# Output projection of a hybrid decoder layer as seven products of halves (Strassen's scheme), with the memory branch in front of it in an order by keys

## Chip, core and metric

The kernel runs on one core of one Trainium2 chip. The metric is the device time of one execution in microseconds (us), lower is better. The engines are TensorE (PE: matmuls; PEld: its weight loads), VectorE (DVE), ScalarE (ACT), GpSimd (POOL) and SyncE (SP), each with a queue of its own that runs in order. SP issues nearly all DMAs.

## What is computed

One decoder layer for 512 tokens and 1024 channels: three branches (SSD, RG-LRU, memory cross-attention) are projected, gated and added; the sum goes through the output projection, the residual is added, and a last RMSNorm is taken. The part that the change touches:

```python
merged = (gates[:, :, 0] * (y_ssd @ w_br_ssd[l])
          + gates[:, :, 1] * (y_lru @ w_br_lru[l])
          + gates[:, :, 2] * (y_mem @ w_br_mem[l]))
x = x + merged @ w_out[l]            # (512, 1024) @ (1024, 1024)
...
return rms_norm(x, final_g)
```

## The kernel before

All matrix products are made in three passes: each operand is split into a high part of type fp32r and the rest (`hi`, a cast on ACT; `lo`, a subtraction `src - hi` on POOL or DVE), and TensorE adds up hi x hi, hi x lo and lo x hi (`mm3`, L279 to L281; `rows_proj`, L300 to L302). One matmul has 128 contracted channels, 128 stationary and 512 moving columns.

Weights come through `WeightStream`: a list of pieces of 128x1024 elements, each loaded by a DMA on SP into one of four `raw` tiles (L83), cast on ACT into `whi` (L100) and subtracted into `wlo` on POOL, POOL, DVE in turn (L102). There are three buffers for `whi` and `wlo`; taking piece i (`ws.next()`) writes out the split of piece i+2 ahead of the matmuls of piece i.

The stage that is changed is the last one. Everything in front of it (SSD, RG-LRU, attention, the sigmoid gates) is the same instruction stream on every engine in both kernels.

- **Memory branch** (L1093 to L1105): for each of eight tiles `ct` of 128 channels TensorE makes 24 matmuls into one PSUM bank (`pj`, four of them). DVE multiplies the result by its gate (L1098, one operand in PSUM, one in SBUF) and adds it to `merged` (L1099, both in SBUF). ACT casts `merged` to its high part (L199), DVE subtracts the low part (L200, both operands in SBUF). The weights are eight pieces of `w_br_mem`.
- **Output projection** (L1128 to L1146): `merged` holds channels on partitions and 512 tokens along the row, so it is the stationary side, four chunks of 128 tokens. The left half of the 1024 output columns is made by `rows_proj` from four pieces of `w_out` (96 matmuls); the right half chunk by chunk, 24 matmuls each, from `woh` and `wol`, which lie in the buffers of the normed input (`hTh`, `hTl`), free by then. That is 8 x 24 = 192 matmuls.
- **End** (`half_done`, L1114): per chunk and half DVE adds the residual (L1117), ACT squares and sums (L1119), DVE multiplies by the gain (L1125); after the right half POOL takes the power -0.5 (L1124), DVE and ACT scale one half each (L1143, L1145), and SP sends both out (L1144, L1146).

The order here is the scheduler's. The RG-LRU stage ahead of it has its order by hand: steps are put into an `Order` list with a key (a time planned by the author) and written out sorted by key, between `tc.manual_schedule()`; the planned lengths in it are keys and hold nothing back.

Of the kernel before, what the change touches and what calls it, by code (L numbers as in the profile page):

```python
# [38 lines left out]
class WeightStream:  # L39
# [50 lines left out]
    def advance(self, upto):  # L90
        while self.n_sub <= min(upto, len(self.subs) - 1):
# [4 lines left out]
            src = self.raw_tiles.pop(i)  # L96
# [52 lines left out]
def kernel(  # L149
# [850 lines left out]
    with tc.tile_pool(name="att", bufs=1, reuse_waits="tile") as ap, ExitStack() as ctx2:  # L1000
# [42 lines left out]
        with tc.tile_pool(name="att2", bufs=1, reuse_waits="tile") as bp:  # L1043
# [48 lines left out]
            mhl = []  # L1092
            for ct in range(KD):  # L1093
                hi, lo = ws.next()
                pt = ps("pj", 4)
# [12 lines left out]
        xr = ap.tile([P, NCH, D], F32, tag="tbx", name="xr")  # L1108
        nc.sync.dma_start(xr, x2.rearrange("(c p) d -> p c d", p=P))
        gb = op.tile([P, D], F32, name="fgb")  # L1110
        nc.sync.dma_start(gb, final_g.partition_broadcast(P))
        stats = [op.tile([P, 4], F32, name=f"ost{c}") for c in range(NCH)]

        def half_done(c, i, pt):  # L1114

            xc, st = xr[:, c, i * 512:(i + 1) * 512], stats[c]
            V.scalar_tensor_tensor(xc, pt, 0.5, xc, op0=ALU.mult, op1=ALU.add)  # L1117
            junk = op.tile([P, 512], BF16, tag="junk", name=f"oj{c}_{i}")
            A.activation(junk, xc, AF.Square, accum_out=st[:, 0:1])  # L1119
            if i == 0:  # L1120
                V.tensor_scalar(st[:, 1:2], st[:, 0:1], 1.0 / D, EPS, op0=ALU.mult, op1=ALU.add)
            else:
                V.scalar_tensor_tensor(st[:, 2:3], st[:, 0:1], 1.0 / D, st[:, 1:2], op0=ALU.mult, op1=ALU.add)
                G.tensor_tensor(st[:, 3:4], st[:, 2:3], mhalf, op=ALU.pow)  # L1124
            V.tensor_mul(xc, xc, gb[:, i * 512:(i + 1) * 512])  # L1125

        pts = rows_proj(lambda k: tuple(m[:, k % 4, :] for m in mhl[k // 4]), NCH, KD)
        woh = hp.tile([P, KD, 512], F32R, tag="hTh", name="woh")  # L1128
        wol = hp.tile([P, KD, 512], F32R, tag="hTl", name="wol")
        for r in range(4):  # L1130
            wr = rawp.tile([P, 1024], F32, tag="raw", name=f"rawo{r}").rearrange("p (k c) -> p k c", k=2)
# [44 lines left out]
```

## Time and profile before

| | |
|---|---|
| median of 3 runs | 969.37 us (967.92 to 970.47) |
| the profiled execution | 968.6 us, of which 966.6 us are its span |
| TensorE busy in the span | 98% |
| the changed stage | 872.5 to 966.6 us of the span: 94.1 us |
| of it memory branch | 872.5 to 916.1 |
| of it output projection | 916.1 to 959.7 |
| of it after the last matmul | 959.7 to 966.6 |

A row of a timeline gives start and length of one instruction (or of some alike, xN) in us, its engine, line, operation, out<-in and shape, and in brackets how long the engine had been idle and what ended that. The start is when the instruction is at the head of its queue with its semaphores there; if it then has to wait for something else, its length grows. Matmuls overlap: a length of 0.39 with starts 0.227 apart.

### The profile page before, as it was taken

To read this page: it belongs to the slowest core of one execution; us is meant where nothing else is said; L and a number is where in the kernel's file an instruction comes from. 1 tells how busy PE (TensorE), PEld (TensorE's weight loads), DVE (VectorE), ACT (ScalarE), POOL (GpSimd) and SP (SyncE) were. 2 spreads that over 40 slices of the span, in tenths; PEclk is the share of its full clock that TensorE was granted. 3 is DMA by queue.
4 is the path that set the end of the run, shared out by engine and by line. 5 is a ranking of instruction groups with operands and counts; after the bars stand their busy time and mean duration, and the time that the engine had idled before them with its cause. 6 is when DMAs were issued, how large, how long until landed. Compare 5 with 4: busy or idle time off the path is not lost.

```text
span 966.6 us, 11884 instructions
## 1 busy us (share of the span) xinstructions
PE 946.8 (98%) x4504; PEld 783.0 (81%) x4504; DVE 611.6 (63%) x932; ACT 446.0 (46%) x673; POOL 281.5 (29%) x156
## 2 busy tenths in 40 slices
PE   8998999999999999999999999999999999999997
PEld 5787778888888888888888887888888988888885
DVE  4398999868688867555648486867465254314643
ACT  5234435544443433331594967768324354332322
POOL 4333315233323323222002011120383442123321
PEclk9999999999999999999999999999999999999999
DMA  7324324333333333324553837464353454233332
GB/s 250 99 68 132 110 66 141 89 110 108 99 103 112 113 94 113 88 69 108 140 155 87 216 112 189 123 169 134 96 165 98 141 159 110 57 99 90 119 119 87
DMA packets 138141, 114.49 MB, mean 118 GB/s; under 512 B 8741, under 2 KB 121701, under 8 KB 138086
## 3 DMA queue, kind: packets, MB, share of 16 engines
q1 hardware_dynamic: 138084, 113.75, 40.6%
q8 instruction: 35, 0.57, 0.2%
q14 instruction: 20, 0.16, 0.1%
q10 hardware_dynamic: 2, 0.00, 0.0%
HBM read 98.99 MB, written 2.16 MB: 105 GB/s over the span
## 4 chain that ended last, share of the span: by engine, by line
PE 84%; DVE 10%; DMA 2%; ACT 1%; issue 1%; POOL 0%; POOLq 0%; SPq 0%; ACTq 0%; DVEq 0%
PE pj L280 21%; PE pj L279 21%; PE pj L281 21%; PE pj L302 2%; PE pj L300 2%; PE pj L301 2%; PE yd L652 2%; DMA m<-acs_d 2%; DVE m L606 2%; DVE cv_xs L310 1%; PE pj L418 1%; PE st L279 1%; PE pj L420 1%; PE pj L419 1%; DVE wlo L102 1%
## 5 line engine op out<-in xcount | busy, mean ns | idle before, releaser
L102 POOL TENSOR_TENSOR wlo<-raw,whi 128x1024 fp32r<-128x1024 f32 (+1 forms) x88 | 211.0, 2399 | 429.3 <-ACT whi L100 419.9
L100 ACT CAST whi<-raw 128x1024 fp32r<-128x1024 f32 (+1 forms) x152 | 155.5, 1025 | 201.9 <-PE pj L280 99.2
L279 PE MATMUL pj<-hTh,whi 128*128 128x512 f32 x624 | 244.6, 392 | 0.2 <-DVE z L317 0.2
L281 PE MATMUL pj<-hTh,wlo 128*128 128x512 f32 x624 | 244.1, 391 | 0.0
L280 PE MATMUL pj<-hTl,whi 128*128 128x512 f32 x624 | 243.8, 391 | 0.0
L279 PEld LDWEIGHTS pj<-hTh,whi 128*128 128x128 f32 x624 | 117.3, 188 | 24.5 <-DVE z L317 0.4
L281 PEld LDWEIGHTS pj<-hTh,wlo 128*128 128x128 f32 x624 | 117.2, 188 | 24.4
L280 PEld LDWEIGHTS pj<-hTl,whi 128*128 128x128 f32 x624 | 117.2, 188 | 24.2
L102 DVE TENSOR_TENSOR wlo<-raw,whi 128x1024 fp32r<-128x1024 f32 x64 | 84.6, 1322 | 55.3 <-ACT whi L100 55.3
L281 PE MATMUL pj<-yTh,wlo 128*128 128x512 f32 x128 | 51.0, 398 | 0.0
L280 PE MATMUL pj<-yTl,whi 128*128 128x512 f32 x128 | 50.5, 394 | 0.0
L279 PE MATMUL pj<-yTh,whi 128*128 128x512 f32 x128 | 50.5, 398 | 0.0
L606 DVE TENSOR_SCALAR m<-m,acs 128x128 f32<-128x128 f32 x128 | 37.7, 362 | 7.5 <-DMA m<-acs_d 7.5
L310 DVE SCALAR_TENSOR_TENSOR cv_xs<-pj,par,cv_xs 128x511 f32<-128x511 f32 (+2 forms) x48 | 35.6, 741 | 9.0 <-ACT cv_xs L307 8.8
L301 PE MATMUL pj<-wlo,hTh 128*128 128x512 f32 x96 | 37.7, 392 | 0.0
L300 PE MATMUL pj<-whi,hTh 128*128 128x512 f32 x96 | 37.5, 398 | 0.0
L302 PE MATMUL pj<-whi,hTl 128*128 128x512 f32 x96 | 37.5, 393 | 0.0
L281 PE MATMUL pj<-lyh,wlo 128*128 128x512 f32 x96 | 37.4, 390 | 0.0
L280 PE MATMUL pj<-lyl,whi 128*128 128x512 f32 x96 | 37.4, 390 | 0.0
L279 PE MATMUL pj<-lyh,whi 128*128 128x512 f32 x96 | 37.4, 390 | 0.0
L652 PEld LDWEIGHTS yd<-xdt,m 128*128 128x128 f32 x256 | 34.5, 191 | 2.4
L652 PE MATMUL yd<-xdt,m 128*128 128x64 f32 x256 | 33.1, 266 | 0.0
(373 smaller groups left out, 1787.1 us busy)
## 6 DMA issues: line engine op xcount, KB each, us to landing
raw<-in_w_in_dram SPq DMA_DIRECT2D x92, 512.0 KB, 3.9
m<-acs_d SPq DMA_DIRECT2D x16, 512.0 KB, 3.7
raw<-in_w_br_ssd_dram SPq DMA_DIRECT2D x16, 512.0 KB, 3.3
raw<-in_w_kv_dram SPq DMA_DIRECT2D x16, 512.0 KB, 3.8
raw<-in_w_br_lru_dram SPq DMA_DIRECT2D x16, 384.0 KB, 3.6
raw<-in_w_br_mem_dram SPq DMA_DIRECT2D x8, 512.0 KB, 3.8
b<-lx SPq DMA_DIRECT2D x8, 384.0 KB, 4.6
ri<-g SPq DMA_DIRECT2D x8, 384.0 KB, 3.7
```

The lines of the kernel that those rows point to most:

```text
L100: self.nc.scalar.copy(hi, src)
L102: lo_engine.tensor_sub(lo, src, hi)
L279: T.matmul(dst, lhsT=lh, rhs=rh, start=(i == 0), stop=False)
L280: T.matmul(dst, lhsT=lh, rhs=rl, start=False, stop=False)
L281: T.matmul(dst, lhsT=ll, rhs=rh, start=False, stop=(i == n - 1))
L300: T.matmul(pts[c], lhsT=lh[:, sl], rhs=hi[:, k2, :], start=first, stop=False)
L301: T.matmul(pts[c], lhsT=lh[:, sl], rhs=lo[:, k2, :], start=False, stop=False)
L302: T.matmul(pts[c], lhsT=ll[:, sl], rhs=hi[:, k2, :], start=False, stop=last)
L310: V.scalar_tensor_tensor(acc[:, k:S], pt[:, 0:S - k], wcol(t), acc[:, k:S], op0=ALU.mult, op1=ALU.add)
L418: T.matmul(zps[c], lhsT=hTh[:, k, sl], rhs=zh[:, k2, :], start=(k == 0), stop=False)
L606: V.tensor_scalar(m[:, h, :], m[:, h, :], acs[:, r0 + h:r0 + h + 1], 0.0, op0=ALU.subtract, op1=ALU.min)
L652: T.matmul(pd[:, h * 64:(h + 1) * 64], lhsT=e["m%d" % c][:, h, :], rhs=e["xdt%d" % c][:, h * 64:(h + 1) * 64], start=True, stop=True)
```

## The change

The 512x1024 matrix `merged` and the 1024x1024 matrix `w_out` are cut into halves both ways: A11, A12 (first 256 tokens), A21, A22 (last 256), B11 to B22. In place of eight products of blocks there are seven, with sums of blocks as operands (Winograd's form): S1 = A21+A22, S2 = S1-A11, S3 = A11-A21, S4 = A12-S2; T1 = B12-B11, T2 = B22-T1, T3 = B22-B12, T4 = T2-B21. The products, in their order: A11 B11, S3 T3, S1 T1, A12 B21, S2 T2, S4 B22, A22 T4. Each is two banks of 128 tokens by 512 columns, made in two parts of 12 matmuls: 7 x 24 = 168 matmuls. The results are added into the residual `xr` quarter by quarter, some by way of a tile `u`.

- `w_out` is no longer streamed: four DMAs of 1 MB bring it as fp32 into the buffers of `hTl` and `hTh` (`wcol`), T1 to T4 are made there in place or in `t3`, and the fourteen half operands run through the weight stream as pieces without a load (`add_kept`): `whi` on ACT, `wlo` on POOL for the first half and on DVE for the second.
- `half_split` follows each memory tile on DVE and ACT: for tiles 0 to 3 the split of A11's part and S3 with its split, for tiles 4 to 7 S1, S2, S4 and three splits. The tiles come in the order 0, 4, 1, 5, 2, 6, 3, 7.
- The whole stage is put into an `Order` list by keys and written out in `manual_schedule`.
- The last scaling is cut at column 640 (DVE) and the rest (ACT), and ACT issues the DMA of its part itself.

The core of the diff:

```diff
+    def add_kept(self, make, k, w, lo_engine):
+        self.lo_of[len(self.subs)] = lo_engine
+        self.subs.append((make, k, w))
...
-            src = self.raw_tiles.pop(i)
+            src = self.subs[i][0]() if callable(self.subs[i][0]) else self.raw_tiles.pop(i)
...
+    for i, ct in enumerate(ct_order):
+        ws.lo_now = (V, G)[i % 2]
+        ws.add_cols(w_mem2, ct * P, 1)
...
+    for i, name in enumerate(("b11", "t3", "t1", "b21", "t2", "b22", "t4")):
+        for r in range(2):
+            ws.add_kept(lambda name=name, r=r: wo[name](r), 2, 512, (G, V)[r])
...
+        def wo_load(l, j):
+            if j == 1:
+                wcol.append(hp.tile([P, KD, 512], F32, tag=("hTl", "hTh")[l], name=f"wcol{l}"))
+            nc.sync.dma_start(wcol[1 - l][:, 4 * j:4 * j + 4, :],
+                              w_out2[j * 512:(j + 1) * 512, l * 512:(l + 1) * 512].rearrange("(k p) c -> p k c", p=P))
...
+        def sum_t3(r):
+            G.tensor_sub(t3[:, 2 * r:2 * r + 2, :], b(1, 1, r), b(0, 1, r))
+        def sum_t1(r):
+            G.tensor_sub(b(0, 1, r), b(0, 1, r), b(0, 0, r))
+        def make_t2(r):
+            V.tensor_sub(b(0, 0, r), b(1, 1, r), b(0, 1, r))
+            return b(0, 0, r)
+        def make_t4(r):
+            (G, V)[r].tensor_sub(b(1, 0, r), b(0, 0, r), b(1, 0, r))
+            return b(1, 0, r)
...
+        def half_split(ct):
+            m = merged[:, ct, :]
+            t0, t1 = m[:, 0:HALF_T], m[:, HALF_T:S]
+            if ct < 4:
+                split(a11[:, 0, ct, :], a11[:, 1, ct, :], t0, V)
+                d = op.tile([P, HALF_T], F32, tag="sd", name=f"sd{ct}")
+                V.tensor_sub(d, t0, t1)
+                split(s3[:, 0, ct, :], s3[:, 1, ct, :], d, V)
+                return
+            j = ct - 4
+            d = op.tile([P, 2, HALF_T], F32, tag="ss", name=f"ss{ct}")
+            V.tensor_add(d[:, 0, :], merged[:, j, HALF_T:S], t1)
+            V.tensor_sub(d[:, 1, :], d[:, 0, :], merged[:, j, 0:HALF_T])
+            split(s12h[:, j], s12l[:, j], d, V)
+            d4 = op.tile([P, HALF_T], F32, tag="sd", name=f"sd{ct}")
+            V.tensor_sub(d4, t0, d[:, 1, :])
+            split(a2h[:, j, :], a2l[:, j, :], m, V)
+            split(s4[:, 0, j, :], s4[:, 1, j, :], d4, V)
...
+            o.at(end + 0.1, done)
+            o.at(end + 1.6, lambda: half_split(ct))
...
+            V.tensor_scalar_mul(xc[:, 0:n], xc[:, 0:n], r)
+            A.mul(xc[:, n:D], xc[:, n:D], r)
+            nc.sync.dma_start(out2[c * P:(c + 1) * P, 0:n], xc[:, 0:n])
+            nc.scalar.dma_start(out2[c * P:(c + 1) * P, n:D], xc[:, n:D])
...
+        def m1(t, pt):
+            A.mul(late["u"][:, t, :], pt, 0.5)
+            G.tensor_add(quarter(0, 0, t), quarter(0, 0, t), late["u"][:, t, :])
...
+        def m6(t, pt):
+            add(late["u"][:, t, :], pt)
+            G.tensor_add(quarter(0, 1, t), quarter(0, 1, t), late["u"][:, t, :])
+        def m7(t, pt):
+            add(late["u"][:, t, :], pt)
+            V.tensor_add(quarter(1, 1, t), quarter(1, 1, t), late["u"][:, t, :])
+            G.tensor_add(quarter(1, 0, t), quarter(1, 0, t), late["u"][:, t, :])
```

What stands where, at three places. First DVE in the memory branch, before, two tiles of channels in a row (`wlo` is a weight's low part, `mkl` the low part of `merged`):

```order
L1098 SCALAR_TENSOR_TENSOR tb_mem<-tb_mem,pj_7264 128x512
L1099 TENSOR_TENSOR merged<-merged,tb_mem 128x512
L102 TENSOR_TENSOR wlo_7298<-raw_7194,whi_7297 128x1024
L200 TENSOR_TENSOR mkl_7292<-merged,mkh_7291 128x512
L1098 SCALAR_TENSOR_TENSOR tb_mem<-tb_mem,pj_7301 128x512
L1099 TENSOR_TENSOR merged<-merged,tb_mem 128x512
L200 TENSOR_TENSOR mkl_7292<-merged,mkh_7291 128x512
```

The same place now, tile 0 from its low part of A11 on and then tile 4 up to the cast S4 waits for (`a` is A11, `sd` S3 or S4 in fp32, `s` its low part, `ss` S1 and S2):

```order
L208 TENSOR_TENSOR a_7262<-merged,a_7262 128x256
L1155 TENSOR_TENSOR sd_7345<-merged 128x256
L208 TENSOR_TENSOR s_7265<-sd_7345,s_7265 128x256
L110 TENSOR_TENSOR wlo_7352<-raw_7226,whi_7351 128x1024
L1182 SCALAR_TENSOR_TENSOR tb_mem<-tb_mem,pj_7315 128x512
L1183 TENSOR_TENSOR merged<-merged,tb_mem 128x512
L1160 TENSOR_TENSOR ss_7384<-merged 128x256
L1161 TENSOR_TENSOR ss_7384<-ss_7384,merged 128x256
L208 TENSOR_TENSOR s12l<-ss_7384,s12h 128x512
L1164 TENSOR_TENSOR sd_7389<-merged,ss_7384 128x256
L208 TENSOR_TENSOR a2l<-merged,a2h 128x512
L208 TENSOR_TENSOR s_7268<-sd_7389,s_7268 128x256
```

Where one subtraction stood behind a tile's addition, three or six instructions stand now, each with two operands in SBUF.

Second, POOL from the weights of the last memory tile on. Before it has the weight pieces and, of `woh` and `wol`, two pieces:

```order
L102 TENSOR_TENSOR wlo_7440<-raw_7330,whi_7439 128x1024
L102 TENSOR_TENSOR wlo_7475<-raw_7365,whi_7474 128x1024
L200 TENSOR_TENSOR wol<-rawo_7662,woh 128x1024
L102 TENSOR_TENSOR wlo_7557<-raw_7437,whi_7556 128x1024
L200 TENSOR_TENSOR wol<-rawo_7670,woh 128x1024
L102 TENSOR_TENSOR wlo_7585<-raw_7472,whi_7584 128x1024
```

Now T3 and T1 stand among the pieces (L1133, L1136), and the additions of the first product (L1275):

```order
L1133 TENSOR_TENSOR t_7269<-wcol_7307 128x1024 x2
L110 TENSOR_TENSOR wlo_7478<-raw_7349,whi_7477 128x1024
L1136 TENSOR_TENSOR wcol_7307<-wcol_7307,wcol_7382 128x1024
L110 TENSOR_TENSOR wlo_7516<-wcol_7382,whi_7515 128x1024
L1136 TENSOR_TENSOR wcol_7307<-wcol_7307,wcol_7382 128x1024
L110 TENSOR_TENSOR wlo_7598<-t_7269,whi_7597 128x1024
L1275 TENSOR_TENSOR xr<-xr,u 128x512
L110 TENSOR_TENSOR wlo_7655<-wcol_7307,whi_7654 128x1024
```

POOL goes from one 1024-wide subtraction for a piece to two for each of four pieces.

Third, POOL ahead of the last product, whose operand T4 is made there (L1143) and split (the last `wlo`); L1286 and L1291 are the additions of the fifth product, which wait for DVE:

```order
L110 TENSOR_TENSOR wlo_7769<-wcol_7307,whi_7768 128x1024
L1286 TENSOR_TENSOR xr<-xr,u 128x512
L1291 TENSOR_TENSOR xr<-xr,u 128x512
L1143 TENSOR_TENSOR wcol_7382<-wcol_7382 128x1024
L110 TENSOR_TENSOR wlo_7815<-wcol_7382,whi_7814 128x1024
L1286 TENSOR_TENSOR xr<-xr,u 128x512
L1291 TENSOR_TENSOR xr<-xr,u 128x512
```

And DVE at the same place, with the second half of T4 (L1143) and its split behind the same additions:

```order
L110 TENSOR_TENSOR wlo_7791<-wcol_7307,whi_7790 128x1024
L1237 SCALAR_TENSOR_TENSOR u<-pj_7766,u 128x512
L1237 SCALAR_TENSOR_TENSOR u<-tr_7652,u 128x512
L1290 TENSOR_TENSOR xr<-xr,u 128x512
L1237 SCALAR_TENSOR_TENSOR u<-pj_7767,u 128x512
L1237 SCALAR_TENSOR_TENSOR u<-yo_7653,u 128x512
L1290 TENSOR_TENSOR xr<-xr,u 128x512
L1252 TENSOR_TENSOR xr<-xr,fgb 128x512
L1257 TENSOR_SCALAR ost_7272<-ost_7272 128x1
L1252 TENSOR_TENSOR xr<-xr,fgb 128x512
L1143 TENSOR_TENSOR wcol_7382<-wcol_7382 128x1024
L110 TENSOR_TENSOR wlo_7844<-wcol_7382,whi_7843 128x1024
```

Before, nothing of this stood there: the last weights had been split by then.

## Rows read from the trace of the kernel before

**Rows 1.** The page: busy time of each engine, share of span, instructions.
```profile
PE 946.8 (98%) x4504; PEld 783.0 (81%) x4504; DVE 611.6 (63%) x932; ACT 446.0 (46%) x673; POOL 281.5 (29%) x156
```
**Rows 2.** By stretch: length, busy PE, PEld, DVE, ACT, POOL, clock, DMA.
```profile
872.50:916.10 43.60, 43.60 (x194) 36.12 (x193) 24.69 (x24) 14.27 (x18) 15.68 (x6) 1.00 0.32 102
916.10:937.90 21.80, 21.80 (x98) 18.06 (x97) 8.91 (x9) 6.82 (x9) 7.15 (x3) 1.00 0.40 148
937.90:959.70 21.80, 21.80 (x97) 17.72 (x95) 9.16 (x22) 6.04 (x15) 2.79 (x3) 1.00 0.19 72
959.70:966.60 6.90, 0.00 (x0) 0.00 (x0) 1.94 (x4) 1.44 (x3) 0.93 (x1) 0.69 0.20 77
```
**Rows 3.** Timeline of TensorE: first matmul of the stage, and a late one.
```profile
872.50 0.39 PE L279 MATMUL pj<-myh,whi 128*128 128x512 f32 x1
...
959.31 0.39 PE L281 MATMUL pj<-woh,mvl 128*128 128x512 f32 x1
```
**Rows 4.** Timeline of DVE and then POOL, second and third memory tile.
```profile
880.61 0.68 DVE L200 TENSOR_TENSOR mkl<-merged,mkh 128x512 fp32r<-128x512 f32 x1
...
884.30 0.69 DVE L1099 TENSOR_TENSOR merged<-merged,tb_mem 128x512 f32<-128x512 f32 x1
885.68 2.12 DVE L200 TENSOR_TENSOR mkl<-merged,mkh 128x512 fp32r<-128x512 f32 x1 [0.69 <-ACT mkh L199]
...
884.53 2.72 POOL L102 TENSOR_TENSOR wlo<-raw,whi 128x1024 fp32r<-128x1024 f32 x1 [8.49 <-ACT whi L100]
```
**Rows 5.** Timeline of DVE and POOL: an operand in PSUM.
```profile
849.60 0.69 DVE L200 TENSOR_TENSOR pTl<-yd,pTh 128x512 fp32r<-128x512 f32 x1 [5.13 <-ACT pTh L199]
...
848.67 2.40 POOL L102 TENSOR_TENSOR wlo<-raw,whi 128x1024 fp32r<-128x1024 f32 x1 [14.90 <-ACT whi L100]
```
**Rows 6.** Timeline of POOL and DVE in the SSD stage.
```profile
93.54 4.40 POOL L102 TENSOR_TENSOR wlo<-raw,whi 128x1024 fp32r<-128x1024 f32 x1 [3.49 <-ACT whi L100]
...
93.36 2.34 DVE L609 TENSOR_TENSOR m<-m,cbm 128x1024 f32<-128x1024 f32 x2
```
**Rows 7.** By line and form: busy us, mean ns of one, idle before it.
```profile
L102 DVE TENSOR_TENSOR wlo<-raw,whi 128x1024 fp32r<-128x1024 f32 x3 | 3.7, 1219 | 0.0
...
L1098 DVE SCALAR_TENSOR_TENSOR tb_mem<-tb_mem,pj 128x512 f32<-128x512 f32 x8 | 5.5, 686 | 23.7 <-PE pj L281 23.7
...
L200 DVE TENSOR_TENSOR kl<-pj,kh 128x256 fp32r<-128x256 f32 x8 | 3.4, 421 | 7.6 <-ACT kh L199 7.6
...
L100 ACT CAST whi<-raw 128x1024 fp32r<-128x1024 f32 x10 | 10.5, 1053 | 29.9 <-PE pj L280 23.0 <-issue 6.9
...
L199 ACT CAST mkh<-merged 128x512 fp32r<-128x512 f32 x4 | 2.5, 620 | 2.4 <-DVE merged L1099 2.4
...
L199 ACT CAST wd<-wdt 128x256 fp32r<-128x256 f32 x1 | 0.4, 395 | 0.0
```
**Rows 8.** Lines L102 and L636 on POOL: ns min/median/max, first and last start.
```profile
L102 POOL TENSOR_TENSOR wlo<-raw,whi x88: 1838/2400/4397, 31.1 to 924.2; 128x1024 fp32r<-128x1024 f32 x72, 128x768 fp32r<-128x768 f32 x16
...
L636 POOL TENSOR_TENSOR prev<-prev,cdb x8: 1044/1047/1952, 109.7 to 383.2; 128x512 f32<-128x512 f32 x8
```
**Rows 9.** Timeline of DVE, ACT, POOL and SP behind the last matmul.
```profile
959.74 0.69 DVE L1117 SCALAR_TENSOR_TENSOR xr<-pj,xr 128x512 f32<-128x512 f32 x1 [2.21 <-PE pj L281]
...
961.36 0.69 DVE L1125 TENSOR_TENSOR xr<-xr,fgb 128x512 f32<-128x512 f32 x1
...
960.52 0.63 ACT L1119 ACTIVATE oj<-xr 128x512 bf16<-128x512 f32 x1 [2.75 <-DVE xr L1117]
961.06 0.19 ACT L1119 ACTIVATION_READ_ACCUMULATOR oj<-xr 128x1 f32 x1
962.48 0.72 ACT L1145 ACTIVATE xr<-xr,ost 128x512 f32<-128x512 f32 x1 [1.24 <-POOL ost L1124]
...
961.52 0.93 POOL L1124 TENSOR_TENSOR ost<-ost,mhalf 128x1 f32<-128x1 f32 x1 [4.51 <-DVE ost L1123]
...
963.43 0.38 SPq L1146 DMA_DIRECT2D out_dram<-xr  x1
```

More of the change, by code (lines that the diff above doesn't have):

```diff
@@ L1107 @@
-        op = ctx2.enter_context(tc.tile_pool(name="outp", bufs=1, reuse_waits="tile"))
[L1108 to L1111, printed above, removed]
-        stats = [op.tile([P, 4], F32, name=f"ost{c}") for c in range(NCH)]
[L1114 to L1131, printed above, removed]
-            nc.sync.dma_start(wr, w_out2[r * 256:(r + 1) * 256, 512:1024].rearrange("(k p) c -> p k c", p=P))
-            k2 = slice(2 * r, 2 * r + 2)
-            split(woh[:, k2, :], wol[:, k2, :], wr, (G, V)[r % 2])
@@ new lines, with product, pe @@
+        o.at(o.t + 1.5, x_load)
+        stats = [op.tile([P, 4], F32, name=f"ost{c}") for c in range(NCH)]
+        def product(lhs, *steps):
+            tags = (("pj", "pj"), ("tr", "yo"), ("pj", "pj"), ("st", "yd"), ("pj", "pj"), ("pj", "pj"), ("tr", "yo"))[product.n]
+            product.n += 1
+            pts = []
+            def pe(r):
+                if r == 0:
+                    pts.extend(ps(tag, 4 if tag == "pj" else 1) for tag in tags)
+                hi, lo = ws.next()
+                for t in range(2):
+                    for k2 in range(2):
+                        lh, ll = lhs(2 * r + k2, slice(t * P, (t + 1) * P))
+                        T.matmul(pts[t], lhsT=lh, rhs=hi[:, k2, :], start=(r == k2 == 0), stop=False)
+                        T.matmul(pts[t], lhsT=lh, rhs=lo[:, k2, :], start=False, stop=False)
+                        T.matmul(pts[t], lhsT=ll, rhs=hi[:, k2, :], start=False, stop=(r == k2 == 1))
+            o.pe(PART, lambda: pe(0))
+            end = o.pe(PART, lambda: pe(1))
+            for t in range(2):
+                for delay, fn in steps:
+                    o.at(end + 0.1 - (1 - t) * PART / 2 + delay, lambda t=t, fn=fn: fn(t, pts[t]))
+            return pts
@@ new lines, with quarter, add, half_steps @@
+        product.n = 0
+        def quarter(i, l, t):
+            return late["x"][:, 2 * i + t, l * 512:(l + 1) * 512]
+        def add(dst, src, scale=0.5):
+            V.scalar_tensor_tensor(dst, src, scale, dst, op0=ALU.mult, op1=ALU.add)
+        def half_steps(i, l, second):
+            def part(t):
+                return late["x"][:, 2 * i + t, l * 512:(l + 1) * 512], stats[2 * i + t]
+            def square(t, _):
+                xc, st = part(t)
+                junk = op.tile([P, 512], BF16, tag="junk", name=f"oj{2 * i + t}_{l}")
+                A.activation(junk, xc, AF.Square, accum_out=st[:, 0:1])
+            def gain(t, _):
+                xc, st = part(t)
+                V.tensor_mul(xc, xc, late["gb"][:, l * 512:(l + 1) * 512])
+            def mean(t, _):
+                xc, st = part(t)
+                if not second:
+                    V.tensor_scalar(st[:, 1:2], st[:, 0:1], 1.0 / D, EPS, op0=ALU.mult, op1=ALU.add)
+                else:
+                    V.scalar_tensor_tensor(st[:, 2:3], st[:, 0:1], 1.0 / D, st[:, 1:2], op0=ALU.mult, op1=ALU.add)
+                    G.tensor_tensor(st[:, 3:4], st[:, 2:3], mhalf, op=ALU.pow)
+            steps = [(0.7, square), (0.7, gain), (1.7, mean)]
+            return steps + [(2.9, lambda t, _: row_done(2 * i + t))] if second else steps
```

104 lines of the change are left out of this document (75 added, 29 removed).

## The prediction

> **What bounds the kernel now.** I read the page first, then the stretches of the last stage, then the timelines of its engines. TensorE is busy 98% of the span [rows 1], and in the last stage 100% from the first memory matmul to the last of the projection, 872.5 to 959.7 [rows 2]: 384 matmuls (8 x 24 and 192), 0.227 us apart [rows 3]. VectorE (DVE) is busy for about half of that and GpSimd (POOL) for under a third [rows 2]. So the stage is bound by TensorE, and taking matmuls out of it pays only while the others keep up. After the last matmul come 6.9 us of end work [rows 2].
>
> Then I look at what DVE and POOL do to each other, since the change gives both more. The low part at 880.61 takes 0.68 us. The same instruction at 885.68 takes 2.12, because POOL subtracts from 884.53 to 887.25: it ends 0.55 behind POOL [rows 4]. All 21 DVE instructions of this kind in the execution (tensor-tensor, 512 columns, both operands in SBUF) that start well inside a long POOL instruction end behind it, by 0.55 in the median. With one operand in PSUM, DVE isn't held: 0.69 in the middle of a POOL subtraction [rows 5]. POOL waits as well: 2.72 in place of 2.40 behind the addition at 884.30 [rows 4, 8], and 4.40 behind two DVE instructions in a row [rows 6]. So two-SBUF-operand work on DVE and POOL's work exclude each other, and their times add up. Before, this sum is small beside TensorE's time.
>
> **What the change removes.** 192 matmuls become 168: 24 x 0.227 = 5.4 us of TensorE. The two DMAs at the end no longer stand behind each other on SP (at most 0.4 [rows 9]). The four 1 MB loads of the projection's weights go into SP's queue among the memory weights; those are taken several tiles later, so I price them at nothing, and at one raw tile's landing (some us, once) if that cover is gone.
>
> **What it adds, part A: up to the split of B22's second half.** Time t runs from the first memory matmul. Work that excludes each other until then, DVE first:
> - nine weight pieces at 1.22 [rows 7] = 11.0, T2's two halves, as wide, 2.4;
> - eight additions to `merged` at 0.69 [rows 4] = 5.5;
> - `half_split`: tiles 0 to 3 have three instructions of 256 columns, tiles 4 to 7 four, and two of 512. For 256 columns the nearest row is 0.42 (its operand is in PSUM) [rows 7], for 512 it is 0.68 [rows 4]: 4 x 1.26 + 4 x 3.04 = 17.2;
> - two gains at 0.69 = 1.4.
>
> That is 37.5. POOL: nine pieces, T3 and T1 in two halves each, 13 x 2.40 [rows 8] = 31.2, and two additions of 512 columns, nearest row 1.05 [rows 8], 2.1: 33.3. Together 70.8. One DVE piece (1.2) goes before the first memory tile ends at 5.5; nothing else is ready earlier, so A is at least 5.5 + 69.6 = 75.1. TensorE alone would begin the sixth product at 43.6 + 5 x 5.44 = 70.8. So even packed without a hole this work is late.
>
> It can't be packed so. DVE's queue is in order, and in it stand the 14 additions out of PSUM (0.69 each, 0.61 of the queue) and, inside each `half_split`, two waits for a cast on ACT: 0.40 twice, or 0.62 and 0.40 [rows 7], each with some 0.12 of hand-over. That is 8.5 + 9.2 = 17.7 more, less what POOL covers with work of its own: A lies between 75.1 and 92.8. POOL has one piece at a time, and often the next one waits for an ACT cast that itself stands behind casts that wait for DVE. I wrote the rows of the four queues down one behind another, each at the latest of its queue, its operands and the excluding engine: that comes to t = 88, and I take it. By that layout TensorE first waits at t = 45, for the low part of B11.
>
> The Trainium skill has a rule on this (SBUF — State Buffer, section "Who interferes with whom"): a DVE instruction with two SBUF inputs contends with a GpSimd instruction that reads SBUF, whoever starts first holds the pair of ports for its whole instruction, and one SBUF input doesn't contend. The trace agrees, with 2.12 against 0.68 and 0.69 beside POOL. If the two only ran side by side, A would be near 72.
>
> **Part B: from there to the second half of T4.** This is a chain from queue to queue that nothing shortens: the additions of the fifth product (S2 T2) and of the second (S3 T3) pass through one tile `u`, POOL's queue has T4's first half between the two tiles' additions, and T4's second half stands on DVE behind all of them. In order: DVE into `u` 0.69, POOL adds 1.05, DVE into `u` again (it must wait for POOL's read) 0.69, POOL adds 1.05, DVE's addition 0.56 behind POOL's end, POOL makes T4's first half 2.40, ACT casts 1.05 [rows 7], POOL subtracts 2.40, POOL adds for the second tile 1.05, DVE into `u` 0.69, POOL 1.05, DVE 0.56, ACT squares 0.82 and DVE multiplies by the gain 0.69 [rows 9], DVE makes T4's second half 1.22, ACT casts 1.05, DVE subtracts 1.22. Sum 18.2, and 13 hand-overs of about 0.06 make it 19.0. TensorE has 12 matmuls to do behind it (2.7), beside the next part.
>
> **Part C: the end.** DVE has been kept from the sixth product's result by part B, so two rounds of end work follow each other, each for two tiles of tokens. One round: add 0.69, square 0.82 on ACT, gain 0.69 (2.2 with hand-overs, since the gain overwrites what ACT squares), then for the second tile add, square, gain 0.69, scale of the first tile about 0.5, statistic 0.16, power 0.93 on POOL, scale 0.6: 4.5. That is 6.7, twice 13.4. From the end of the last scaling (963.20) to the end of the span are 3.4 [rows 9, 2], less up to 0.4 for the second queue: 3.3.
>
> **The sum.** 88 + 19.0 + 13.4 + 3.3 = 123.7, against 94.1 before (872.5 to 966.6): +29.6. The profiled execution takes 968.6, 2.0 over its span, so 998.2; the median of the runs, 969.37, is 0.8 above that execution: 999.0. With A at its ends the stage takes 110.8 or 128.5: 986 to 1004.
>
> **Rivals.**
> - *DVE and POOL get along* (same order, little exclusion; each works in the other's holes). For it: many DVE instructions read PSUM, and POOL is idle for long now. Against: the 21 rows. Then A is about 72, with parts B and C as they are: 107.7, +13.6, so 983.
> - *TensorE stays the bound, faster.* The keys place every sum behind its product, and if DVE, ACT and POOL follow them, the stage is 5.4 shorter in matmuls and about 1.0 longer at its end (the second tile's 4.5 and 3.3 against 6.9): 965. It decides by whether T4's second half is split by t = 43.6 + 6.5 x 5.44 = 79.0. For that part A would have to end by 60, which is below its 75.1, or part B to be done beside other work, which its order excludes.
> - *TensorE's clock falls as well.* The granted clock is 1.00 (2.4 GHz) in every stretch with matmuls and 0.69 on average in the last, where none runs and it goes to the lower level, 1.2 GHz [rows 2]. The change makes TensorE wait up to 4 or 5 us at a time. At the lower level a matmul would take 0.45, and the sixth product would begin at 43.6 + 5 x 10.9 = 98, not 88: +10, so 1009. The Trainium skill (TensorE: Matmul & The Clock Gate, section "HAM oscillation — how this bites in real kernels") tells of kernels that throttle at each wait for data and start every piece cold; no row here shows a wait between matmuls at a lower clock.
>
> **Chances.** The forecast, slower by some 30 us, 0.78; DVE and POOL get along 0.12; the clock falls 0.06; TensorE stays the bound 0.04. The predicted time is 999. The range goes from 983 (the second case, below part A's lower end) to 1007. A measurement of this kernel can tell about 0.3% (2.9 us) from no change. Faster by more 0.04, within it 0.01, slower 0.95.
>
> **What would show it.** In the profile of the changed kernel: the memory branch's 192 matmuls still without waits, in about 44 us; the 168 of the products over some 65 us in place of 38, with waits for `wlo` and `whi`; DVE's 256-column instructions in the memory branch at over 2 us where POOL runs, 0.42 elsewhere; the longest waits, about 4.5 us, in front of the two halves of the last product; some 14 us from the last matmul to the end in place of 6.9. The prediction is wrong if those DVE instructions stay near 0.42 beside POOL (then 983), if the products run at 0.227 per matmul (then 965), or if the granted clock falls below 1.00 among them (then more than 1004).

## The result, and the profile after

| | before | changed |
|---|---|---|
| median on the same chip | 969.53 us (4 runs, 967.92 to 970.47) | 996.29 us (4 runs, 995.85 to 998.07) |
| ratio | 1 | 1.0294, interval 1.0272 to 1.0315 |
| the profiled execution, of it span | 968.6, 966.6 | 996.7, 995.0 |
| the last stage | 872.5 to 966.6: 94.1 | 871.7 to 995.0: 123.3 |
| of it up to the first product | 43.6 | 43.7 |
| of it to the end of the matmuls | 43.6 | 69 |
| of it after the matmuls | 6.9 | 10.6 |

The change makes the kernel 2.9% slower. Times here and below are medians of undisturbed executions; of the kernel fill (run 1) one execution of four took 3346 us and is left out. Of the page, the row of busy time answers to [rows 1]. Its columns are busy time, share of the span and instructions:

```profile
PE 951.9 (96%) x4480; PEld 781.5 (79%) x4480; DVE 648.5 (65%) x976; ACT 456.1 (46%) x693; POOL 306.0 (31%) x168
```

TensorE has 24 matmuls less and is "busy" 5 us longer (some of them ran at the lower clock level, below). DVE has 37 us more. The page's shares still look like a kernel that TensorE bounds; only the stretches of the last stage show that it no longer does. Stretches of the changed kernel, cut at the points that the prediction's parts use, with the columns of [rows 2] (length, busy PE, PEld, DVE, ACT, POOL, granted clock, DMA):

```profile
871.80:915.40 43.60, 43.60 (x194) 35.92 (x192) 33.07 (x36) 12.90 (x20) 17.39 (x7) 1.00 0.39 128
915.40:960.40 45.00, 35.52 (x129) 26.16 (x129) 33.30 (x39) 17.14 (x25) 20.27 (x9) 0.89 0.17 59
960.40:979.30 18.90, 9.84 (x30) 6.56 (x28) 8.66 (x13) 3.44 (x6) 10.74 (x6) 0.78 0.00 1
979.30:991.40 12.10, 5.06 (x11) 3.47 (x11) 7.51 (x17) 5.18 (x12) 2.20 (x4) 0.64 0.31 119
```

In the first stretch TensorE is full, as before, but DVE is busy for 33.1 us in place of 24.7 [rows 2]. In the second neither is full, and DVE and POOL together are busy for 53.6 of 45.0 us (time in which an instruction is held counts as busy). In the third TensorE works for half of the time, and in the fourth less. The waits of TensorE over the whole stage (line waited for: us in total, times, longest) name most of the operands it lacked:

```profile
PE tr L1222 <- ACT whi L108: 8.8, 3, 4.2
PE pj L1222 <- ACT whi L108: 3.8, 1, 3.8
PE pj L1223 <- POOL wlo L110: 1.7, 3, 1.0
```

These are weight pieces of the seven products, `whi` and `wlo`; of `merged` it waited for one half operand, `a`, for 0.5 us. Before, no matmul of this stage waited. The chain that ended last, from 955 on (start us, length, engine, tile, line), holds no TensorE at all; from the first product to there it holds 7 us of it (936.3 to 943.4). Here is its part that makes T4:

```profile
961.03 1.30 POOL xr L1286
...
962.36 0.70 DVE u L1237
...
963.13 1.78 POOL xr L1291
964.91 2.31 POOL wcol L1143
...
967.24 1.05 ACT whi L108
...
968.36 2.35 POOL wlo L110
970.71 1.24 POOL xr L1286
...
971.98 0.70 DVE u L1237
...
...
975.75 1.15 DVE wcol L1143
...
976.97 1.05 ACT whi L108
...
978.05 1.23 DVE wlo L110
```

That is the order that part B of the prediction wrote down: two additions of POOL with DVE's `u` between them, T4's first half (L1143, then its cast and split), the second tile's `u`, and T4's second half on DVE at the end of it.

What DVE and POOL do to each other stands in the memory branch. Timeline of DVE, then of POOL, in the changed kernel (columns as in [rows 4]):

```profile
879.21 2.06 DVE L208 TENSOR_TENSOR a<-merged,a 128x256 fp32r<-128x256 f32 x1 [0.47 <-ACT a L207]
881.20 0.41 DVE L1155 TENSOR_TENSOR sd<-merged 128x256 f32<-128x256 f32 x1
...
895.72 2.62 DVE L1155 TENSOR_TENSOR sd<-merged 128x256 f32<-128x256 f32 x1
...
878.23 2.76 POOL L110 TENSOR_TENSOR wlo<-raw,whi 128x1024 fp32r<-128x1024 f32 x1 [8.45 <-ACT whi L108]
890.32 2.39 POOL L110 TENSOR_TENSOR wlo<-raw,whi 128x1024 fp32r<-128x1024 f32 x1 [9.34 <-ACT whi L108]
892.67 5.39 POOL L1133 TENSOR_TENSOR t<-wcol 128x1024 f32<-128x1024 f32 x2
```

A 256-column subtraction takes 0.41 us at 881.20, where POOL has just ended, and 2.06 at 879.21, inside POOL's split: it ends at 881.27, 0.3 behind POOL. The same line as the free one takes 2.62 at 895.72, behind POOL's two halves of T3. By line and form over the whole stage (busy us, mean ns of one), two of the forms that meet POOL:

```profile
L1183 DVE TENSOR_TENSOR merged<-merged,tb_mem 128x512 f32<-128x512 f32 x8 | 14.2, 1770 | 0.3
L208 DVE TENSOR_TENSOR a<-merged,a 128x256 fp32r<-128x256 f32 x4 | 6.6, 1654 | 1.9 <-ACT a L207 1.9
```

The additions to `merged` need 1.77 us in the mean, where a free one takes 0.69 [rows 4].

Held instructions of this kind lie on the chain that ended last. From 882.6 to 936 it holds only DVE and the casts on ACT, no POOL instruction and no matmul. Five pieces of it:

```profile
890.42 2.85 DVE merged L1183
...
893.74 2.06 DVE a L208
895.80 2.55 DVE sd L1155
...
913.76 2.88 DVE merged L1183
...
916.67 2.51 DVE ss L1160
```

Three more follow the same pattern: 2.85 us at 906.52 (`merged`), 2.06 at 909.83 (`a`) and 2.85 at 928.07 (`merged`). The free pieces of the same lines on this chain take 0.70 (`merged`), 0.43 (`a`), 0.35 (`sd`) and 0.44 (`ss`), so the eight are longer by 16.2 us in sum.

### The profile page after: what moved, and what is told of

Its sections match the earlier page's. It is cut to its first block, busy times and chain, and to the rows that moved or that the text cites. A ratio compares the mean times of both kernels' runs of the same rounds, so it can differ in the third digit from the quotient of the medians.

```text
span 995.0 us, 11923 instructions
## 1 busy us (share of the span) xinstructions
PE 951.9 (96%) x4480; PEld 781.5 (79%) x4480; DVE 648.5 (65%) x976; ACT 456.1 (46%) x693; POOL 306.0 (31%) x168
## 4 chain that ended last, share of the span: by engine, by line
PE 75%; DVE 16%; ACT 3%; DMA 3%; issue 2%; POOL 2%; SPq 0%; POOLq 0%; ACTq 0%; DVEq 0%
PE pj L287 19%; PE pj L288 19%; PE pj L289 19%; DMA m<-acs_d 2%; PE yd L666 2%; DVE m L620 2%; PE pj L310 2%; PE pj L308 2%; PE pj L309 2%; DVE wlo L110 1%; DVE merged L1183 1%; DVE cv_xs L318 1%; ACT whi L108 1%; PE st L287 1%; PE st L288 1%
## 5 line engine op out<-in xcount | busy, mean ns | idle before, releaser
L110 POOL TENSOR_TENSOR wlo<-raw,whi 128x1024 fp32r<-128x1024 f32 (+1 forms) x84 | 200.9, 2393 | 428.9 <-ACT whi L108 419.5
L108 ACT CAST whi<-raw 128x1024 fp32r<-128x1024 f32 (+1 forms) x148 | 151.3, 1024 | 179.4 <-issue 81.0
L287 PEld LDWEIGHTS pj<-hTh,whi 128*128 128x128 f32 x624 | 117.3, 188 | 24.7 <-DVE z L325 0.6
L799 POOL TENSOR_TENSOR gwl<-gw,gwh 96x768 fp32r<-96x768 f32 x4 | 7.4, 1848 | 87.0 <-ACT gwh L795 87.0
```

Of the source, the lines that this page charges most:

```text
L108: self.nc.scalar.copy(hi, src)
L110: lo_engine.tensor_sub(lo, src, hi)
L287: T.matmul(dst, lhsT=lh, rhs=rh, start=(i == 0), stop=False)
```

## Experiments

All times are medians beside the kernel before on the same chip, which there had 968.0 to 969.3. The table cuts the stage of each kernel as the prediction does: A from the first memory matmul to the end of DVE's split of B22's second half, B from there to the end of its split of T4's second half, and the rest to the end of the span. The points are read from the timelines of the profiled executions (changed kernel: 871.7, 959.14 + 1.21, 978.05 + 1.23, 995.0).

| kernel | A | B | rest | stage | time | over before |
|---|---|---|---|---|---|---|
| changed | 88.7 | 18.9 | 15.7 | 123.3 | 996.3 | +26.8 |
| fill | 72.7 | 18.1 | 15.7 | 106.4 | 980.4 | +12.3 |
| all-dve | 84.5 | 15.4 | 15.7 | 115.6 | 986.4 | +18.3 |
| chain | 90.9 | 12.1 | 15.7 | 118.7 | 992.6 | +24.4 |
| warm | 88.3 | 19.0 | 15.7 | 123.0 | 997.7 | +29.5 |
| no-t | 77.7 | 13.1 | 15.7 | 106.5 | 981.3 | +13.2 |
| no-s | 74.3 | 18.9 | 15.9 | 109.0 | 983.9 | +14.5 |
| no-sums | 71.7 | 13.0 | 15.9 | 100.6 | 975.5 | +7.4 |
| best | 84.7 | 11.2 | 16.0 | 111.9 | 985.7 | +16.3 |

TensorE alone would begin the sixth product at 70.8, so an A of about 71 or 72 means that TensorE sets the pace up to there.

### 1. POOL writes only (fill)

The theory: part A is long because the work of DVE and POOL excludes each other. The rival: part A is the sum of queues and hand-overs, and would be as long beside a POOL that disturbs nobody.

```diff
-            lo_engine.tensor_sub(lo, src, hi)
+            if lo_engine is self.nc.gpsimd and i >= self.dull:
+                for part in (lo, lo, lo[:, 0:k // 2, :]):
+                    lo_engine.memset(part.bitcast(F32), 0.0)
+            else:
+                lo_engine.tensor_sub(lo, src, hi)
...
-            G.tensor_sub(t3[:, 2 * r:2 * r + 2, :], b(1, 1, r), b(0, 1, r))
+            for k in (2, 2, 1):
+                G.memset(t3[:, 2 * r:2 * r + k, :], 0.0)
```

> The changed kernel, but GpSimd's 1024-wide subtractions of the last stage (nine weight pieces, T3, T1, T4's first half) only fill their targets: 2.5 fills of 1024 columns each, meant to last about as long, and reading nothing from SBUF. Those low parts and sums are left out of the computation. Theory (VectorE's work on two SBUF operands and GpSimd's reading work exclude each other): VectorE's 256-column instructions stay at 0.42 us beside GpSimd, the split of B22's second half ends at about t = 73 in place of 88, the whole takes about 980 us (977 to 985). Rival (GpSimd's queue is simply late, whatever it does to VectorE): VectorE's instructions beside GpSimd may be short, but the waits stay; the low parts no longer wait for ScalarE's cast, which gives a few us: 990 to 997 us.

Measured: 980.44 us, ratio 1.0131 (1.0102 to 1.0161). POOL is about as long at each place as in the changed kernel, and DVE's instructions beside the fills have their free length. Timeline of DVE, then POOL, and the additions to `merged` by form, in this kernel:

```profile
879.80 0.42 DVE L213 TENSOR_TENSOR a<-merged,a 128x256 fp32r<-128x256 f32 x1 [0.47 <-ACT a L212]
...
877.94 2.56 POOL L113 MEMSET wlo<- 128x1024 f32 x3 [7.57 <-PE pj L294]
...
L1195 DVE TENSOR_TENSOR merged<-merged,tb_mem 128x512 f32<-128x512 f32 x8 | 5.5, 692 | 0.3
```

The subtraction at 879.80 lies inside POOL's fills (877.94 to 880.50), as the one at 879.21 of the changed kernel lies inside its subtraction, and takes 0.42 in place of 2.06. The additions to `merged` add up to 5.5 us in place of 14.2, the 28 instructions of 256 columns to 11.8 in place of 21.0, and A falls from 88.7 to 72.7, TensorE's own pace. B is 18.1 in place of 18.9. The rival falls. One difference more: the fills read neither source nor `whi`, so POOL no longer waits for the cast in front of its pieces. The chain of the changed kernel says how little of A's 16.0 us that can be: up to 956 no POOL instruction lies on it, and the eight held instructions of DVE, with 16.2 us, are enough for the whole difference.

The Trainium skill (SBUF — State Buffer, section "Who interferes with whom") says that DVE's instructions with two SBUF inputs contend with a GpSimd instruction that reads SBUF and not with one that only writes it. The two traces agree: 2.06 us beside a subtraction, 0.42 beside a fill.

### 2. All of POOL's work on DVE (all-dve)

```diff
-        ws.lo_now = (V, G)[i % 2]
+        ws.lo_now = V
...
-            ws.add_kept(lambda name=name, r=r: wo[name](r), 2, 512, (G, V)[r])
+            ws.add_kept(lambda name=name, r=r: wo[name](r), 2, 512, V)
...
-            (G, V)[r].tensor_sub(b(1, 0, r), b(0, 0, r), b(1, 0, r))
+            V.tensor_sub(b(1, 0, r), b(0, 0, r), b(1, 0, r))
...
-            G.tensor_add(quarter(0, 0, t), quarter(0, 0, t), late["u"][:, t, :])
+            V.tensor_add(quarter(0, 0, t), quarter(0, 0, t), late["u"][:, t, :])
```

T1, T3 and the other additions of `u` move in the same way. If POOL really worked beside DVE, taking its 51 us away and loading DVE with them would cost a lot.

> The changed kernel with all of GpSimd's work of the last stage (low parts, T sums, additions into the residual; not the power) moved to VectorE, the busier of the two. Theory (the times of the two add up, and a piece takes 2.40 us on GpSimd and 1.22 on VectorE): the sum of excluding work shrinks, 87 to about 66 us, so faster than the changed kernel by about 9 us: 987 (983 to 991), still slower than before. Rival (each engine bound by its own load, no exclusion): 15 pieces of 1.22 and 6 additions more on VectorE make it slower, by 8 us or more: over 1003.

Measured: 986.43 us, ratio 1.0195 (1.0167 to 1.0223). Over the kernel before that is 8.5 us less than the changed kernel (by the two ratios 9.6, and the stage is 7.7 shorter), with the same sums and, but for the power, one engine less. One stretch of this kernel (columns as above):

```profile
915.00:965.00 50.00, 40.68 (x151) 30.03 (x150) 36.97 (x50) 16.55 (x25) 0.00 (x0) 0.90 0.15 53
```

So POOL's help in this stage was worth less than nothing. A piece takes 1.22 us on DVE and 2.40 on POOL [rows 7, 8], and while POOL takes its 2.40, DVE's two-operand work stands. DVE is busy for 37.0 of 50 us here; in the changed kernel it was 36.2 of the same 50 (row with run 4), with less work, stretched by POOL. A falls by 4.2 and B by 3.5; the gain in B needn't be exclusion, since the pieces of its chain are shorter on DVE in any case.

### 3. Part B's chain cut (chain)

The fifth product's sum gets a tile of its own (`u3`), and T4 is made in the middle of the fifth product, ahead of the additions out of `u`.

```diff
-            add(late["u"][:, t, :], pt)
-            V.tensor_add(quarter(1, 1, t), quarter(1, 1, t), late["u"][:, t, :])
-            G.tensor_add(quarter(1, 0, t), quarter(1, 0, t), late["u"][:, t, :])
+            V.scalar_tensor_tensor(late["u3"][:, t, :], pt, 0.5, late["u"][:, t, :], op0=ALU.mult, op1=ALU.add)
+            V.tensor_add(quarter(1, 1, t), quarter(1, 1, t), late["u3"][:, t, :])
+            G.tensor_add(quarter(1, 0, t), quarter(1, 0, t), late["u3"][:, t, :])
...
+        for r in range(2):
+            o.at(8 * PROJ + 2 * PART * (4 + 0.5 * r) + 0.01, lambda r=r: sum_t4(r))
```

> The changed kernel with part B's chain cut in two places: the second product's addition goes into a tile of its own (u3), so VectorE needn't wait for GpSimd's read of u, and T4 is made in the middle of the fifth product, ahead of those additions. Same amount of work. Theory (part B is a chain from queue to queue, 19 us): some 5 us less, 991 (988 to 994), with the waits in front of the last product shorter. Rival (the excluding work alone sets the time, wherever it stands): within 1.5 us of 996.

Measured: 992.59 us, ratio 1.0254 (1.0219 to 1.029). By its time over before this is 2.4 us closer to the kernel before than the changed one (by the ratios 3.9), while the two intervals overlap; the profile, whose stage is 4.6 shorter, separates them: B is 12.1 in place of 18.9, and A is 2.2 longer. DVE and POOL at the end of A in this kernel:

```profile
960.83 3.35 DVE L110 TENSOR_TENSOR wlo<-wcol,whi 128x1024 fp32r<-128x1024 f32 x1
...
960.26 2.85 POOL L1146 TENSOR_TENSOR wcol<-wcol 128x1024 f32<-128x1024 f32 x1
```

T4's first half now stands beside the split of B22's second half, which is held: 3.35 us in place of 1.21. So the chain was on the path, 6.8 us of it went, and a third came back as exclusion. Which of the two edits gave how much, this run doesn't show.

### 4. The clock kept up (warm)

In the changed kernel the granted clock falls to the lower level, 1.2 GHz, four times among the products. Stretches of the changed kernel (columns as above):

```profile
915.40:923.20 7.80, 3.44 (x13) 2.17 (x12) 6.57 (x8) 2.49 (x4) 3.49 (x2) 1.00 0.00 0
923.20:930.00 6.80, 5.50 (x13) 3.64 (x12) 5.79 (x8) 1.75 (x3) 2.00 (x1) 0.50 0.00 0
930.00:936.90 6.90, 4.25 (x17) 2.73 (x16) 4.96 (x8) 4.46 (x8) 1.76 (x2) 0.99 0.69 221
936.90:940.30 3.40, 3.40 (x10) 2.62 (x9) 2.47 (x1) 0.90 (x1) 3.40 (x3) 0.51 0.82 324
940.30:967.60 27.30, 22.71 (x98) 17.81 (x96) 16.06 (x20) 7.90 (x11) 14.99 (x7) 1.00 0.00 1
967.60:974.40 6.80, 4.43 (x10) 3.11 (x11) 2.39 (x3) 2.04 (x5) 5.23 (x3) 0.50 0.00 0
974.40:977.80 3.40, 0.84 (x4) 0.36 (x2) 2.48 (x4) 0.83 (x1) 0.13 (x1) 1.00 0.01 2
977.80:984.60 6.80, 5.86 (x12) 3.76 (x12) 4.47 (x9) 2.19 (x6) 0.93 (x2) 0.50 0.04 16
```

Each fall follows a stretch in which TensorE waited for weight halves. Does the low level cost time? This run puts 16, 12, 16 and 12 matmuls for nothing, into a bank that isn't in use then, ahead of the second halves of the first and second product and of both halves of the last, where TensorE waits anyway:

```diff
+                n = {(1, 1): 16, (2, 1): 12, (7, 0): 16, (7, 1): 12}.get((number, r), 0)
+                if n:
+                    idle = ps("st")
+                    for i in range(n):
+                        T.matmul(idle, lhsT=a11[:, 0, 0, 0:P], rhs=a2h[:, 0, :], start=(i == 0), stop=(i == n - 1))
```

> The changed kernel with matmuls for nothing (results dropped) ahead of four parts at which TensorE waits longest: 16 ahead of the second half of the first product, 12 of the second's, 16 and 12 ahead of the halves of the last, 0.227 us each, less than the waits. Theory (TensorE isn't the bound, so its lower clock level costs next to nothing): the granted clock is back near 1.00 among the products and the time within 2 us of 996. Rival (the clock is part of the loss): the 24 us at 1.2 GHz are worth up to 12, so 984 to 991 us.

Measured: 997.71 us, ratio 1.0308 (1.0283 to 1.0332), no faster than the changed kernel. The same two stretches, first of the changed kernel, then of this one:

```profile
915.00:965.00 50.00, 39.70 (x146) 29.13 (x144) 36.24 (x42) 17.14 (x25) 23.83 (x12) 0.90 0.15 53
965.00:990.00 25.00, 11.13 (x24) 7.22 (x24) 12.97 (x23) 8.00 (x17) 9.22 (x7) 0.69 0.11 42
```

```profile
915.00:965.00 50.00, 44.38 (x181) 34.27 (x180) 37.29 (x42) 17.18 (x25) 24.25 (x11) 0.97 0.14 53
965.00:990.00 25.00, 14.39 (x52) 9.88 (x50) 12.26 (x22) 7.88 (x17) 9.96 (x8) 0.85 0.11 43
```

The clock rises from 0.90 to 0.97 and from 0.69 to 0.85; two short stretches at the lower level remain, 6.8 us together in place of 23.8. A, B and the rest are within 0.4 of the changed kernel's. Where TensorE waits for DVE, ACT and POOL, a slower matmul only fills a part of the wait. One of the four stretches, 936.9 to 940.3, lies on the chain, where half of its 3.4 us could count, 1.7 at most; this run has such a stretch as well (931.5 to 934.9), so it does not settle that one.

### 5. Which sums cost what (no-t, no-s, no-sums)

No-t uses blocks of `w_out` in place of T1 to T4, no-s blocks of `merged` in place of S1 to S4 (as operands and without their extra splits), no-sums both. The products, their additions and the end stay. The core of the edits:

```diff
-            if n in (3, 4):
-                o.at(end - PROJ + 2.5, lambda: sum_t3(n - 3))
-            if n in (5, 6):
-                o.at(end - PROJ + 2.5, lambda: sum_t1(n - 5))
...
-            split(a2h[:, j, :], a2l[:, j, :], m, V)
-            split(s4[:, 0, j, :], s4[:, 1, j, :], d4, V)
+            split(a2h[:, ct - 4, :], a2l[:, ct - 4, :], m, V)
```

> The changed kernel with T1 to T4 alone left out of the computation (plain blocks of w_out in their place); S1 to S4 and half_split stay. Four 2.40 us sums on GpSimd (T3, T1), T4's two halves and T2's two on VectorE go: 12.0 us of GpSimd and 3.7 of VectorE. Theory (this work excludes the rest and adds up): 15.7 us less and a little more from the chain of part B, 980 us (977 to 984). Rival (GpSimd's sums lie beside VectorE's work and only T2 and T4 stand in a chain): 990 us or more.

> The changed kernel with S1 to S4 alone left out of the computation: half_split is one split of 512 columns per memory tile, the products take plain blocks of merged. T1 to T4 stay. On VectorE 17.2 us become 8 x 0.68 = 5.4, and eight of the sixteen waits for a cast on ScalarE go. Theory (excluding work adds up, waits inside half_split count as well): 11.8 us less work and some of the waits, less what GpSimd's T sums then still hold up: 984 us (980 to 988). Rival (the part of VectorE that goes was beside GpSimd's work anyway): 992 us or more.

> The changed kernel with all sums of operands left out of the computation: S1 to S4 and T1 to T4 are plain blocks, half_split is one split of 512 columns per memory tile as before, GpSimd and VectorE make no T. The 168 matmuls, the 14 pieces of w_out, the additions into the residual and the order stay. Theory (the excluding work sets the time up to the sixth product, then the chain of part B, then two rounds of end work): the work falls to TensorE's size and part A is over with TensorE, but the chain through u with GpSimd's pieces in it and the doubled end remain: 974 us (970 to 977), still slower than before. Rival (the sums are the whole loss, and without them the 24 matmuls show): 965 us.

Measured: 981.25 us (ratio 1.0146, 1.0126 to 1.0167), 983.85 (1.0145, 1.0122 to 1.0169) and 975.45 (1.0084, 1.0066 to 1.0102). Without the T sums the time over before falls by 13.6 us, without the S sums by 12.3, without both by 19.4. They overlap by 6.5, since with either set gone A already comes near TensorE's own pace (77.7 and 74.3).

The most telling of the three is no-sums. Even with no sum of blocks to make, seven products in place of eight blocks' worth are 7.4 us slower than before. Its A is 71.7, so up to there TensorE sets the pace. B is 13.0, since DVE's second round with `u` waits for POOL's split between POOL's additions. POOL and then DVE in this kernel:

```profile
948.37 2.34 POOL L110 TENSOR_TENSOR wlo<-wcol,whi 128x1024 fp32r<-128x1024 f32 x1
...
951.99 0.69 DVE L1216 SCALAR_TENSOR_TENSOR u<-yo,u 128x512 f32<-128x512 f32 x1 [4.13 <-POOL xr L1265]
```

And its end is the doubled one. The last matmul starts at 959.34 and the span ends 13.5 us later; before, it is 7.3 (959.31 [rows 3] to 966.6). Its last matmul starts 87.2 us after the stage's first, before 86.8: the saved 5.4 us of matmuls is used up ahead of the end, and the 6.2 us of longer end are nearly all of its loss.

### 6. The two edits with no sums in them (order, end)

Order is the kernel before with its memory branch alone written out in a fixed order; end is the kernel before with the last scaling cut at 640 and ACT issuing the second DMA.

```diff
+            with tc.manual_schedule():
+                mhl = []
+                for ct in range(KD):
+                    hi, lo = ws.next()
```

```diff
-            nc.sync.dma_start(out2[c * P:(c + 1) * P, 512:1024], xr[:, c, 512:1024])
+            A.mul(xr[:, c, 640:D], xr[:, c, 640:D], stats[c][:, 3:4])
+            nc.sync.dma_start(out2[c * P:(c + 1) * P, 0:640], xr[:, c, 0:640])
+            nc.scalar.dma_start(out2[c * P:(c + 1) * P, 640:D], xr[:, c, 640:D])
```

> The kernel before with the memory branch alone in a fixed order (as written, tiles 0 to 7), the projection in eight products as it was. Theory: TensorE has no wait in that stage before or with it, so no change: within 1.5 us of before. Rival (part of the loss is the fixed order): 2 us or more slower than before.

> The kernel before with the change's end alone: the last scaling cut at column 640 and ScalarE issuing the second DMA of each chunk. Theory: the last DMA is issued some 0.3 us earlier, at most 0.5 us of the whole, which can't be told from no change. Rival (the second queue makes the last transfers themselves faster): 1 us or more less.

Measured: 968.56 us, ratio 1.0011 (0.9996 to 1.0026), and 968.52, ratio 1.0002 (0.9989 to 1.0014). Neither the order by hand of the memory branch nor the new end moves the time by an amount that can be told from none, so the 2.9% aren't theirs. With the runs above that leaves the products in halves and their sums; the order of the tiles and the new split of the weight pieces between POOL and DVE have no run of their own.

### 7. Both cures together (best)

All of POOL's work on DVE as in run 2, with `u3` and the early T4 of run 3; nothing is left out.

> The whole scheme, nothing left out, with what the runs so far point to: all of GpSimd's work of the stage on VectorE, u3 as a tile of its own, T4 made in the middle of the fifth product. Theory: the two gains overlap, since the chain held GpSimd's instructions; 984 us (981 to 987), still slower than before, because VectorE then has about 80 us of work for TensorE's 82 and begins 5 us later. Rival (with both causes gone the 24 matmuls show): 965 us.

Measured: 985.66 us, ratio 1.0171 (1.0148 to 1.0194). B falls to 11.2, but A stays at 84.7: what is left there is DVE's own queue. A stretch of it:

```profile
915.00:965.00 50.00, 40.09 (x157) 29.61 (x156) 39.09 (x53) 17.56 (x26) 0.00 (x0) 0.96 0.14 53
```

DVE is busy for 39.1 of 50 us and waits for casts in the rest. No version of the scheme that was run comes near the kernel before.

## Why the prediction was right, point by point

- **TensorE no longer bounds the stage.** Held. The first wait, for the low part of B11, begins 43.9 us after the stage's first matmul (forecast 45), the memory branch runs without waits in 43.6 (forecast about 44), and the products take 69 (forecast 65). In front of the halves of the last product TensorE waits 4.2 and 2.8 us (forecast about 4.5, as the longest of all; one of 3.8 stands in the first product).
- **Part A, exclusive work of DVE and POOL.** Forecast 88, measured 88.7. That exclusion makes it so long is shown by run 1 (72.7 without it, as the rival "get along" had priced it), by the 16.2 us of held time on the chain and, from the other side, by run 2, where A falls by 4.2 with POOL's work moved to DVE. The 256-column instructions went over 2 us beside POOL as said. The layout of the four queues that gave 88 isn't written out, so only its bounds (75.1 and 92.8) can be followed; the measured time lies between them. Two things the layout did not name: the additions to `merged` were held more than any others (14.2 us in place of 5.5), and most of POOL's own pieces and sums took 2.5 to 2.8 in the mean rather than 2.40.
- **Part B, the chain through `u` to T4.** Forecast 19.0, measured 18.9, and run 3 shows that it is on the path. Inside it two errors cancel: POOL's additions took 1.27 to 1.78 where 1.05 was forecast (the row came from another stage), and T4's first half started at 964.87, at the end of POOL's second addition, without the 0.56 for DVE's that the sum had put in front of it. That the sum is right to 0.1 us is in part luck; the chain is right.
- **Part C, two rounds of end work.** The mechanism held, the size was off: 12.1 (979.3 to 991.4) in place of 13.4. The mis-sized term is the power on POOL, 0.93 [rows 9], twice on the path. In the changed kernel it takes 0.55 each of four times:

```profile
988.19 0.55 POOL L1260 TENSOR_TENSOR ost<-ost,mhalf 128x1 f32<-128x1 f32 x1 [3.42 <-DVE ost L1259]
...
988.89 0.69 DVE L1252 TENSOR_TENSOR xr<-xr,fgb 128x512 f32<-128x512 f32 x1 [0.78 <-ACT oj L1248]
```

  The first of these ends at 988.74, before DVE's next gain starts. Before, the gain at 961.36 covers the start of the power at 961.52 [rows 9], and the power ends 0.40 behind it. So 0.93 was a held length, by the prediction's own rule, taken for a free one. The kernel before shows it in its SSD stage too, where the same power runs beside other work (POOL, then DVE):

```profile
117.22 0.93 POOL L666 TENSOR_TENSOR rs<-st,mhalf 128x1 f32<-128x1 f32 x1 [3.52 <-PE pj L281]
148.78 0.55 POOL L666 TENSOR_TENSOR rs<-st,mhalf 128x1 f32<-128x1 f32 x1 [1.28 <-DVE st L664]
...
117.06 0.68 DVE L200 TENSOR_TENSOR xddl<-xdd,xddh 128x512 fp32r<-128x512 f32 x1
148.56 0.68 DVE L618 TENSOR_TENSOR xdt<-tr,dtq 128x512 f32<-128x512 f32 x1
```

  At 117.22 a DVE instruction with both operands in SBUF covers the start, and the power ends 0.41 behind it; at 148.78 one with an operand in PSUM (`tr`) does, and the power takes 0.55. Of the 26 powers of that execution 17 take 0.55; the other nine, 0.93 to 1.53, all end 0.40 to 0.42 behind a DVE instruction of the first kind that had started ahead of them. In part C this is 0.76 of the 1.3; the rest are hand-overs.
- **The rest of the span.** Forecast 3.3, measured 3.6. From the last matmul's start (983.76) to the end are 11.2 us; the forecast was some 14, because TensorE's last 12 matmuls ran at the lower clock and so ended later, beside the end work rather than ahead of it. In run 4, where they ran at the higher level, it is 13.2 (982.51 to 995.7).
- **The sum.** Forecast 123.7 for the stage, measured 123.3. Its parts are off by +0.7, -0.1, -1.3 and +0.3, so it is partly luck that the whole is closer than part C. The remaining 2.7 us between 999.0 and 996.3 are this 0.4, a start of the stage 0.8 earlier, 0.3 less around the span, and 1.2 from how the two profiled executions lie to their medians.
- **"If the granted clock falls below 1.00 among the products, then more than 1004."** Wrong. It fell, for 24 us, and the time stayed at 996. The step that failed is the price of that rival: it put matmuls at 0.45 one behind another (they did run 0.43 apart), as if TensorE were the bound, where the same text had just argued that it would not be. Run 4 shows the low level all but without cost here. The Trainium skill (TensorE: Matmul & The Clock Gate, section "HAM oscillation — how this bites in real kernels") counts half of the throttled time of such a kernel as lost, which for 23.8 us would be an estimated 11.9. The falls after waits agree with it; of the loss this stage shows at most 1.7.
- **The other rivals.** "DVE and POOL get along" is run 1's stage, not this kernel's. "TensorE stays the bound" failed at T4, split at 107.6 where 79.0 was needed; even without any sum (no-sums) it is split at 84.7.
- **Edits costed at nothing.** The fixed order and the new end cost and gave nothing that can be told (runs order and end). The four 1 MB loads among the memory weights were not tried alone; the memory branch shows no wait that would be theirs.

## What to carry to other kernels

Trading matmuls for additions pays only if the engines that add have free time at that place: here 24 matmuls (5.4 us of TensorE) were bought with sums and splits that cost about 19 us, and with a longer end that alone would have eaten the gain. Count the work of DVE with two SBUF operands and the work of POOL that reads SBUF as one queue, and where DVE makes the same piece in half the time, as here, try it without POOL. Price a clock rival, or any slower engine, only for stretches in which that engine is the bound.

## What was not expected of the hardware

- The granted clock went to the lower level in four stretches among the products (23.8 us in sum), and keeping it up for 17 us of these gave nothing (run 4).
- The power on POOL takes 0.55 us when no DVE instruction with two SBUF operands covers its start, and 0.93 to 1.53 in the nine cases of the kernel before in which one does: even a 128x1 instruction of POOL ends behind it, by 0.40 to 0.42.
- Taking POOL out of the stage, but for the power, was faster than using it beside DVE, by some 8.5 us (run 2).
